# A decoder block's FFN output: two groups of nine pairs, with weight sums made ahead in device memory

## The chip, the cores and the metric

The kernel runs on one core of a Trainium2 chip. The metric is the device time of one launch in microseconds. Three runs of the kernel before gave a median of 2124.69 us (2124.45 to 2126.43). The engines are named as in the profile: PE is TensorE's matmul, PEld its weight load, DVE is VectorE, ACT is ScalarE, POOL is GpSimd and SP is SyncE. SP, ACT and POOL also issue DMA transfers, each on a queue of its own.

## The reference

With one layer the reference is a sparse-attention mixer and a SwiGLU FFN over 512 tokens of width 2048, with RMSNorm ahead of each and behind the last. The change is in the last part, the FFN's output and the final norm:

```python
x = x + nsa_mixer(rmsnorm(x, mix_norm_g), ...)           # (512, 2048)
h = rmsnorm(x, ffn_norm_g)
z = h @ w_in                                             # (512, 2 * 5632)
a, b = z[..., :5632], z[..., 5632:]
x = x + (silu(a) * b) @ w_out                            # (512, 5632) @ (5632, 2048)
return rmsnorm(x, final_norm_g)
```

All is float32. The kernel writes each operand as a sum of two float32r parts, high and low, and makes three matmuls of each product (`three`): high by high, high by low, low by high.

## The kernel before, in words

**Stages.** Attention, its output projection (`W_out`), the FFN input (`f_in`), the FFN output (`f_out`). An instruction's place in its engine's order is the order in which the Python code issues it. Splitting an operand takes one ACT copy (the high part) and one DVE subtraction (the low part, helper `sub`, line 1038).

**FFN input** (from about 864 us). 82 units `q`, two to each of 41 column blocks `p`. A unit is a product of the 2 by 2 blocks in seven products instead of eight (Strassen's way in Winograd's form): `split_unit` makes the sums of weight blocks and splits them, `load_unit(q + 3)` loads the weights of a later unit on SP's queue into three `raw` buffers and one `rawx`, `products(q)` issues 84 matmuls of 256 columns, `merge` puts the sums together. Each second `p` ends a pair: `merge` multiplies it by the gate of the block ahead, and `keep_a` stores 128 x 1024 numbers to `d_a` on POOL's queue. The tile that is stored, `E`, has two buffers.

**FFN output** (from about 1660 us). The sum over 5632 goes by 22 pairs `j` of 256, the columns by four blocks `b` of 512: 88 units (b, j), in the order of `ORDER`, block after block. Each block's sums stay in PSUM over its 22 units: four banks `po` and four `qs` for the parts of the seven products.

- A *plain* unit (`plain_tile`) loads its weights (512 KB) and its pair from `d_a` (512 KB, into `rawx` or `tt`), splits both (1024 columns each), and makes 24 matmuls of 512 columns, token tile by token tile.
- A *seven* unit (`seven_unit`, those in `SEVEN[b]`, 44 of the 88) takes seven products by 42 matmuls of 256 columns. Its left factors (four blocks of the pair and sums of them, in two parts of 1792 columns) are made by `form` during the four units ahead, and kept in SBUF for five pairs (`KEPT`); for the others they are stored to `d_s` and loaded again for each block on POOL's queue (`load_seven`). Its right factors are the four weight blocks and three sums of them, `weight_sums`: four DVE operations of 256 columns, and a split of 768.

`W2.take` gives a unit's split weights and splits those of units ahead. The split weights have four buffers, the split `thi`, `tlo` two. Where a seven unit follows a plain one, its split sums lie 32 columns further in their buffer than where it follows a seven (`c0`).

The residual stands in `d_r` and is loaded into `acc` (all four column blocks in SBUF). Behind the last seven unit of a block `merge_sums` adds the parts to `acc`; behind the block's last unit four additions do so with `po`. `ready(b)` then takes the block's sums of squares and multiplies it by the final gain, during the next block.

**The tail.** The last `N_TAIL` = 4 units of the last block are plain ones, taken token tile by token tile: for each tile four units' matmuls, then the addition to `acc` (line 954), sum of squares, gain (line 1559), the reciprocal root, and scaling and output of the four pieces. `last_tile` does the same for the last tile in two halves.

## Time and profile before

| | |
|---|---|
| median of 3 runs | 2124.69 us |
| profiled execution | 2123.49 us, span 2121.8 us, mean granted clock 0.998 |
| TensorE busy | 2098.6 us (99%), 14717 matmuls |
| VectorE busy | 1634.6 us (77%) |
| ScalarE busy | 932.7 us (44%) |
| DMA | 388.08 MB, mean 183 GB/s |

The span is cut into 40 slices of 53 us on the page; the FFN input takes slices 17 to 31 or so, the FFN output those behind. A busy TensorE is not a TensorE at its peak, since matmuls overlap; what one costs is read from the time between two starts. The lines that carry this are in the prediction.

### The profile page before, as it was taken

Reading aid. Unit: us, or ns where it says so; the run is one execution under the profiler, and the core shown is the slowest. Engines: PE = TensorE matmul, PEld = TensorE weight load, DVE = VectorE, ACT = ScalarE, POOL = GpSimd, SP = SyncE. Lnnn points to the kernel's source line nnn. Section 1 sums busy time; section 2 is a strip of 40 time slices with the busy share of each in tenths; the row PEclk is TensorE's granted clock in tenths of the full one; section 3 lists DMA queues with packets and bytes.
Section 4 is the critical chain, followed back from the end, with each engine's and each line's share of the span. In section 5 each row is a group of like instructions: output and inputs, shape, how many; then the busy total and the mean of one; then the engine's idle time right before and its main releaser. Section 6 shows DMA issues by size and latency. Waiting matters only on the chain.

```text
span 2121.8 us, 37227 instructions
## 1 busy us (share of the span) xinstructions
PE 2098.6 (99%) x14717; PEld 1947.1 (92%) x14717; DVE 1634.6 (77%) x2674; ACT 932.7 (44%) x1451; POOL 125.9 (6%) x206
## 2 busy tenths in 40 slices
PE   9999999999989999999999999999999999999998
PEld 7898788898979889999999999999999988999997
DVE  5565777877786366898888888888888787877785
ACT  5344455455554334434344343443434454444344
POOL 1000111111111000000000000000000000001000
PEclk9999999999999999999999999999999999999999
DMA  7555767666676643344344333434344776878893
GB/s 232 174 154 151 192 191 203 185 200 189 194 234 199 243 147 110 121 138 128 122 130 127 122 121 124 135 120 129 116 125 129 267 286 210 305 267 311 308 340 137
DMA packets 273371, 388.08 MB, mean 183 GB/s; under 512 B 34251, under 2 KB 206091, under 8 KB 272556
## 3 DMA queue, kind: packets, MB, share of 16 engines
q1 hardware_dynamic: 248540, 279.98, 42.3%
q0 software_dynamic: 22896, 102.31, 14.0%
q10 hardware_dynamic: 1760, 3.42, 0.4%
q8 instruction: 115, 1.88, 0.4%
q14 instruction: 60, 0.49, 0.1%
HBM read 320.52 MB, written 70.36 MB: 184 GB/s over the span
## 4 chain that ended last, share of the span: by engine, by line
PE 70%; ACT 0%; DVE 0%; issue 0%; ACTq 0%
PE f L268 19%; PE f L269 19%; PE f L270 19%; PE proj L268 2%; PE proj L269 2%; PE proj L270 2%; PE pp L268 1%; PE pp L270 1%; PE pp L269 1%; PE po L268 1%; PE po L269 1%; PE po L270 1%; PE pp L246 0%; PE o L269 0%; PE o L270 0%; PE o L268 0%
## 5 line engine op out<-in xcount | busy, mean ns | idle before, releaser
L98 DVE TENSOR_TENSOR wlo<-raw,whi 128x1024 fp32r<-128x1024 f32 (+1 forms) x225 | 269.3, 1199 | 116.2 <-ACT whi L97 115.9
L97 ACT ACTIVATE whi<-raw 128x1024 fp32r<-128x1024 f32 (+1 forms) x225 | 233.3, 1040 | 222.4 <-DVE raw L1038 123.2
L1038 DVE TENSOR_TENSOR tlo<-tt,thi 128x1536 fp32r<-128x1536 f32 (+2 forms) x135 | 197.1, 1460 | 109.0 <-ACT thi L1143 86.9
L270 PE MATMUL f<-hn_h,wlo 128*128 128x256 f32 x984 | 271.6, 276 | 0.0
L268 PE MATMUL f<-hn_h,whi 128*128 128x256 f32 x984 | 271.6, 276 | 0.0
L269 PE MATMUL f<-hn_l,whi 128*128 128x256 f32 x984 | 271.6, 276 | 0.0
L1138 ACT ACTIVATE whi<-raw 128x1024 fp32r<-128x1024 f32 x123 | 126.0, 1057 | 293.6 <-DVE raw L1038 290.2
L268 PE MATMUL proj<-hn_h,whi 128*128 128x512 f32 x512 | 204.2, 399 | 0.7 <-ACT hn_h L410 0.7
L269 PE MATMUL proj<-hn_l,whi 128*128 128x512 f32 x512 | 200.6, 392 | 0.3 <-DVE hn_l L411 0.3
L270 PE MATMUL proj<-hn_h,wlo 128*128 128x512 f32 x512 | 200.6, 392 | 0.0
L269 PEld LDWEIGHTS f<-hn_l,whi 128*128 128x128 f32 x984 | 184.7, 188 | 0.0
L268 PEld LDWEIGHTS f<-hn_h,whi 128*128 128x128 f32 x984 | 184.7, 188 | 0.0
L270 PEld LDWEIGHTS f<-hn_h,wlo 128*128 128x128 f32 x984 | 184.7, 188 | 0.0
L1143 ACT ACTIVATE thi<-tt 128x1536 fp32r<-128x1536 f32 x82 | 121.9, 1486 | 82.3 <-PE f L269 70.6
L270 PE MATMUL proj<-whi,hn_l 128*128 128x256 f32 (+2 forms) x496 | 145.4, 293 | 3.9 <-DVE hn_l L731 3.9
L1038 DVE TENSOR_TENSOR wlo<-raw,whi 128x1024 fp32r<-128x1024 f32 x123 | 147.0, 1223 | 1.1 <-ACT whi L1138 1.1
L268 PE MATMUL proj<-whi,hn_h 128*128 128x256 f32 (+2 forms) x496 | 145.7, 294 | 0.8 <-ACT hn_h L730 0.8
L269 PE MATMUL proj<-wlo,hn_h 128*128 128x256 f32 (+2 forms) x496 | 144.8, 292 | 0.0
L269 PE MATMUL f<-wlo,thi 128*128 128x512 f32 x320 | 124.9, 390 | 0.0
L270 PE MATMUL f<-whi,tlo 128*128 128x512 f32 x320 | 124.8, 390 | 0.0
L268 PE MATMUL f<-whi,thi 128*128 128x512 f32 x320 | 124.7, 390 | 0.0
L270 PEld LDWEIGHTS proj<-hn_h,wlo 128*128 128x128 f32 x512 | 96.4, 188 | 21.5 <-DVE wlo L98 0.2
(346 smaller groups left out, 6112.2 us busy)
## 6 DMA issues: line engine op xcount, KB each, us to landing
raw<-in_ffn_w_in SPq DMA_DIRECT2D x135, 512.0 KB, 3.7
raw<-in_ffn_w_out SPq DMA_DIRECT2D x88, 512.0 KB, 5.6
rawx<-in_ffn_w_in SPq DMA_DIRECT2D x41, 512.0 KB, 4.8
rawx<-d_a SPq DMA_DIRECT2D x31, 512.0 KB, 5.1
ah<-d_s POOLq DMA_DIRECT2D x16, 896.0 KB, 6.9
al<-d_s POOLq DMA_DIRECT2D x16, 896.0 KB, 9.3
raw<-in_nsa_w_in POOLq DMA_DIRECT2D x24, 512.0 KB, 4.8
raw<-in_nsa_w_in SPq DMA_DIRECT2D x23, 512.0 KB, 5.0
```

Of the source, the lines that this page charges most:

```text
L97: self.nc.scalar.activation(hi[:, :n], src, AF.Copy)
L98: self.nc.vector.tensor_tensor(lo[:, :n], src, hi[:, :n].bitcast(F32), op=OP.subtract)
L268: mm(o, ah, bh, start=start, stop=False, skip_group_check=True)
L269: mm(o, ah, bl, start=False, stop=False, skip_group_check=True)
L270: mm(o, al, bh, start=False, stop=stop, skip_group_check=True)
L1038: dve.tensor_tensor(o, a, b, op=OP.subtract)
L1138: act(h, r, AF.Copy)
L1143: act(h, ttf, AF.Copy)
```

## The change

- **Order.** `PASSES` replaces `ORDER`. Pairs 3 to 11 (`G1`) and 12 to 20 (`G2`) are the two groups. The first three passes take blocks 0, 1 and 2 over pairs 0 to 11 (in part), the fourth takes block 3 over both groups, and the last three take blocks 2, 1 and 0 over pairs 12 to 21 with the rest. The third part of each entry lists the pairs that are plain there; 63 units are seven units. At the end of a pass its block is added to `d_r` in device memory (first three) or the stored sum is added to it in SBUF and the block goes to `ready`, which now takes only the sums of squares and stores it (next three), both by an accumulating DMA on POOL's queue.
- **Left factors.** Each group's nine pairs keep their factors in 18 slots of SBUF (13 on the left side, five on the right). `form` is one generator run over two units: `form_front` issues the sums, `form_back` the ACT copies and, a unit later, the subtractions. The raw pair lands in the slot itself, two pairs ahead (`load_forms`). `d_s` and its traffic are gone.
- **Right factors.** `made_ahead` makes four sums of weight blocks for each of the 18 pairs and all four column blocks in device memory (`d_w`): four copies of 512 KB, then four accumulating transfers of 512 KB in three steps, all on POOL's queue. Its 72 steps are issued among the stages ahead: four beside `W_out`, six beside the first plain units of the FFN input, and three in each four of its units `q` (`PRE`). A seven unit loads 384 KB of plain weights and 512 KB of sums, two units ahead, and splits 768 and 1024 columns; DVE makes no sums of weights.
- **Tail.** Block 0 is the last. Its residual is added by an accumulating DMA into SBUF behind `merge_sums`, just ahead of the last four units. The other three blocks are read back to `ytile` (four loads of 768 KB), and each token tile is multiplied by their gain (1536 columns) in the tail.
- **Places.** New pools and gaps put slots and splits at the same offsets as before modulo 256 bytes.

The diff, cut to its core (left out are loads and splits that change their buffers alone, and names that follow):

```diff
-KEPT = (3, 8, 13, 16, 18)
-SEVEN = [KEPT + x for x in ((6, 11), (6, 11, 0, 1, 2, 4)) + 2 * ((6, 11, 0, 1, 2, 4, 5, 7),)]
-TAIL_LOAD, TAIL_SPLIT = {5: 0, 7: 1, 9: 2, 11: 3}, {7: 0, 9: 1, 13: 2, 15: 3}
-ORDER = [tuple(range(22)),
-         (3, 5, 6, 7, 0, 9, 8, 10, 1, 12, 11, 13, 14, 2, 16, 15, 17, 4, 18, 19, 20, 21),
-         (6, 9, 3, 11, 10, 5, 8, 12, 0, 13, 14, 1, 15, 7, 16, 2, 17, 18, 4, 19, 20, 21),
-         (6, 9, 11, 3, 0, 8, 1, 13, 2, 16, 4, 18, 5, 10, 7, 12, 14, 15, 17, 19, 20, 21)]
+G1, G2 = tuple(range(3, 12)), tuple(range(12, 21))
+PASSES = [(0, (6, 7, 8, 9, 3, 5, 4, 10, 11), (5, 6, 7, 8, 9, 10, 11)),
+          (1, (3, 4, 5, 6, 0, 7, 8, 9, 1, 10, 11), (0, 1, 10, 11)),
+          (2, (3, 4, 5, 6, 0, 7, 8, 9, 10, 11, 1), (0, 1)),
+          (3, (3, 4, 5, 0, 6, 7, 8, 1, 9, 10, 11, 12, 13, 2, 14, 15, 16, 17, 18, 19, 20, 21), (0, 1, 2, 21)),
+          (2, (12, 13, 14, 15, 16, 2, 17, 18, 19, 20, 21), (2, 21)),
+          (1, (12, 13, 14, 15, 16, 2, 17, 18, 19, 20, 21), (2, 21)),
+          (0, (12, 13, 14, 15, 16, 17, 18, 19, 20, 0, 1, 2, 21), (0, 1, 2, 21))]
+N_FIRST, FORM_FROM, PRE = 4, 2, (1, 1, 1, 0)
+UNITS = [(b, j, j not in flat) for b, js, flat in PASSES for j in js]
...
+    def three_of(j, b):
+        return (1, 768, [(0, 256, mat(f_out, 256 * j, 1, 512 * b, 256, D)),
+                         (256, 768, mat(f_out, 256 * j + 128, 1, 512 * b, 512, D))])
...
+    d_w = {j: dram.tile([128, 4, 4, 256], F32, name=f"d_w{j}") for j in G1 + G2}
+
+    def made_ahead():
+
+        for j in G1 + G2:
+            b11, b12, b21, b22 = (bass.AP(tensor=f_out.tensor, offset=f_out.offset + 128 * (2 * j + i) * D + 256 * c,
+                                          ap=[[D, 128], [512, 4], [1, 256]]) for i in range(2) for c in range(2))
+            t1, t3, t2, t4 = (d_w[j][:, :, i] for i in range(4))
+            for o, i in ((t1, b11), (t3, b12), (t2, b11), (t4, b21)):
+                pool.dma_start(o, i)
+            yield
+            pool.dma_start(t1, b12, accum_op=OP.add)
+            pool.dma_start(t3, b22, accum_op=OP.add)
+            yield
+            pool.dma_start(t2, t3, accum_op=OP.add)
+            yield
+            pool.dma_start(t4, t2, accum_op=OP.add)
+            yield
+
+    ready_made = made_ahead()
...
+            next(ready_made)
...
+                    if i != 1:
+                        next(ready_made)
...
+    def split_t(n):
+
+        def rest():
+            c0 = 0 if UNITS[n - 1][2] else 32
+            h, l = (tq.tile([128, 1088], F32R, name=f"t{x}")[:, c0:c0 + 1024] for x in ("hi", "lo"))
+            t = t_raw.pop(n)
+            act(h, t, AF.Copy)
+            sub(l, t, f32(h))
+            t_hl[n] = [x.rearrange("p (n c) -> p n c", n=4) for x in (h, l)]
+
+        return lambda r: rest
...
+        for _ in range(PRE[q % len(PRE)]):
+            next(ready_made, None)
+    run(ready_made)
...
+    def load_forms(n):
+
+        while len(raw_in) < min(len(used), forms["k"] + 2):
+            k = len(raw_in)
+            if k >= 9 and last_use[used[k - 9]] > n - 1 or k in (6, 7, 8) and n < N_FIRST:
+                break
+            raw_in.append((slot_tile(), slot_tile()))
+            nc.sync.dma_start(f32(raw_in[k][1][:, 768:]), d_a[used[k]])
...
+    def form_front(n, quiet):
+
+        k = forms["k"]
+        if forms["at"] or k >= len(used) or n < FORM_FROM:
+            return
+        must = first_use[used[k]] <= n + 2
+        if k >= len(raw_in) or quiet and not must:
+            return
+        forms["it"], forms["at"] = form(k), 1
+        next(forms["it"])
+
+    def form_back(n, quiet):
+
+        if forms["at"] == 1:
+            next(forms["it"])
+            forms["at"] = 2
+            if first_use[used[forms["k"]]] > n + 1:
+                return
+        elif quiet and forms["at"] == 2 and first_use[used[forms["k"]]] > n + 1:
+            return
+        if forms["at"] == 2:
+            next(forms["it"])
+            forms["at"] = 0
+            forms["k"] += 1
...
-        b = [[x[:, i, 256 * c:256 * (c + 1)] for x in w] for i in range(2) for c in range(2)]
-        th, tl = t_hl.pop(n)
-        right = dict(p1=b[0], p5=b[1], p2=b[2], p3=b[3], p7=(th[:, 0], tl[:, 0]), p6=(th[:, 1], tl[:, 1]),
-                     p4=(th[:, 2], tl[:, 2]))
-        for name in ("p7", "p6", "p1", "p5", "p2", "p3", "p4"):
+        t = t_hl.pop(n)
+        right = {p: [x[:, 0, 256 * i:256 * (i + 1)] for x in w] for i, p in enumerate(("p1", "p2", "p3"))}
+        right.update((p, [x[:, i] for x in t]) for i, p in enumerate(("p5", "p7", "p6", "p4")))
+        for name in ("p7", "p6", "p5", "p1", "p4", "p2", "p3"):
...
+    def merge_sums(qs):
+
+        o = accb["now"] = late2.tile([128, NT, 512], F32, name="accb")
+        u2 = late2.tile([128, 1024], F32, name="m")[:, :512]
 
         def halves(x):
             return x.rearrange("p (u c) -> p u c", u=2)
 
-        act(u3, qs["p1"], AF.Copy)
-        plus(u2, u3, qs["p6"])
-        plus(acc[:, :2, c[0]], acc[:, :2, c[0]], halves(u3))
-        plus(u3, u2, qs["p7"])
-        plus(acc[:, 2:, c[0]], acc[:, 2:, c[0]], halves(u3))
-        mm2 = m.rearrange("p (a c) -> p a c", a=2)
-        plus(mm2, mm2, qs["p5"].unsqueeze(1).to_broadcast([128, 2, 512]))
-        plus(acc[:, :, c[1]], acc[:, :, c[1]], m.rearrange("p (t c) -> p t c", t=4))
-
-    def ready(b, gf):
-
-        c = slice(512 * b, 512 * (b + 1))
+        act(o[:, :2, :256], halves(qs["p1"]), AF.Copy)
+        plus(halves(u2), o[:, :2, :256], halves(qs["p6"]))
+        plus(o[:, 2:, :256], halves(u2), halves(qs["p7"]))
+        sub(o[:, :2, 256:], halves(qs["p5"]), halves(u2))
+        sub(o[:, 2:, 256:], halves(qs["p5"]), o[:, 2:, :256])
+
+    def ready(b):
...
+        pool.dma_start(stored(b), o)
+
+    load_forms(0)
+    for i in range(2, N_FIRST + 1):
+        load_t(i)
+    load_a(N_FIRST)
...
+            load_forms(n)
+            form_front(n, quiet)
+            for x in range(W2.ncv, min(n + (4 if left == 0 else 3 if left < 3 else 2), NU)):
+                W2.ahead(x + 1 - W2.nt)
+                load_t(x + 2)
...
+            if last_pass and i == 6:
+                for t in range(NT):
+                    ytile[t] = slot_tile(F32)[:, 48:48 + 1536]
+                    nc.sync.dma_start(ytile[t], d_r[t][:, 512:])
+            if last_pass and i == 7:
+                gf = slot_tile(F32)[:, 48:48 + 512]
+                nc.sync.dma_start(gf, fin_g[None, :512].to_broadcast([128, 512]))
+                gfs = slot_tile(F32)[:, 48:48 + 1536]
+                nc.sync.dma_start(gfs, fin_g[None, 512:].to_broadcast([128, 1536]))
...
+        if last_pass:
+            merge_sums(pending)
+            pool.dma_start(accb["now"], stored(b), accum_op=OP.add)
+            continue
+        o = accb["now"]
+        for t in range(NT):
+            plus(o[:, t], o[:, t], po[t])
+        if s < 3:
+            pool.dma_start(stored(b), o, accum_op=OP.add)
+        else:
+            pool.dma_start(o, stored(b), accum_op=OP.add)
+            todo = ready(b)
...
+    for t in range(NT):
+        if t < NT - 1:
+            for i in range(N_TAIL):
+                if t == 0:
+                    w8.append(W2.take(N_TAIL - 1 - i))
+                plain_tile(n + i, w8[i], t, False, i == N_TAIL - 1)
+        dve.tensor_tensor(ytile[t], ytile[t], gfs, op=OP.mult)
+        if t == NT - 1:
+            break
+        plus(acc[:, t], acc[:, t], po[t])
+        act(po[t], acc[:, t], AF.Square, accum_out=ss[t][:, :1])
+        dve.tensor_tensor(acc[:, t], acc[:, t], gf, op=OP.mult)
...
```

More of the change, by code (lines that the diff above doesn't have):

```diff
@@ L164, in granules @@
         out += [(4, 256, [(0, 256, mat(f_in, 512 * i, 4, ffn_col(p), 256, 2 * DFF))]) for i in range(4)]
-    return out, [rows(f_out, 2 * j, 2, 512 * b, 512) for b in range(4) for j in ORDER[b]], marks, off
+    return out, [three_of(j, b) if seven else rows(f_out, 2 * j, 2, 512 * b, 512) for b, j, seven in UNITS], marks, off
 def ffn_col(p):
@@ L1306, in nsa_block, with load_a @@
-    for n, (b, j) in enumerate(seq):
-        if j in SEVEN[b]:
-            W2.sums[n] = weight_sums(n)
+    NU = len(UNITS)
+    a_raw, a_hl, t_raw, t_hl, slot = {}, {}, {}, {}, {}
+    tq = tp
+    plain_units = [n for n, (_, _, seven) in enumerate(UNITS[:-N_TAIL]) if not seven]
+    def load_a(i):
+        if i < len(plain_units):
+            n = plain_units[i]
+            a_raw[n] = (tp.tile([128, 1024 + 512 * (i % 2)], F32, name=("rawx", "tt")[i % 2], bufs=1)[:, :2 * S]
+                        if n < N_FIRST else tq.tile([128, 1024], F32, name="landp", bufs=1))
+            nc.sync.dma_start(a_raw[n], d_a[UNITS[n][1]])
@@ L1310, in nsa_block @@
+    def split_t(n):
[7 more added lines that the diff above has]
+        return lambda r: rest
+    for n, (_, _, seven) in enumerate(UNITS):
+        if seven:
+            W2.sums[n] = split_t(n)
     for q in range(NQ):
@@ L1333, in nsa_block @@
+    tq = ctx.enter_context(tc.tile_pool(name="tq", bufs=2))
     late2 = ctx.enter_context(tc.tile_pool(name="late2", bufs=1))
     ss = [late2.tile([128, 4], F32, name=f"sf{t}") for t in range(NT)]
[L1335 to L1340 removed]
@@ L1341, in nsa_block, with cols @@
[L1341 to L1352 removed]
+    accb, ytile = {}, {}
+    def cols(b):
+        return slice(512 * b, 512 * (b + 1))
@@ new lines, in stored, with slot_tile @@
+    def stored(b):
+        return d_r[:, :, cols(b)].rearrange("t p c -> p t c")
+    used = [j for js in (G1, G2) for j in js]
+    first_use = {j: n for n, (_, j, seven) in reversed(list(enumerate(UNITS))) if seven}
+    last_use = {j: n for n, (_, j, seven) in enumerate(UNITS) if seven}
+    n_slot = [0]
+    def slot_tile(dtype=F32R):
+        i = n_slot[0] % 18
+        n_slot[0] += 1
+        return (pair_pool if i < 13 else right).tile([128, 1792], dtype, name="slot", bufs=13 if i < 13 else 5)
@@ L1409, in plain_tile, with tail_load, tail_split @@
+    def tail_load(i):
+        n = NU - N_TAIL + i
+        a_hl[n] = [x[:, 48:48 + 2 * S] for x in (slot_tile(), slot_tile())]
+        nc.sync.dma_start(f32(a_hl[n][1]), d_a[UNITS[n][1]])
+    def tail_split(i):
+        h, l = a_hl[NU - N_TAIL + i]
+        act(h, f32(l), AF.Copy)
+        sub(l, f32(l), f32(h))
     def plain_tile(n, w, t, first, last):
@@ L1466, in nsa_block @@
         started = False
         for i, j in enumerate(units):
-            left = len(units) - 1 - i if b == 3 else 9
-            w = W2.take(3 if left == 0 else 2 if left < 3 else 1)
+            left = len(units) - 1 - i if last_pass else 9
+            quiet = i in (0, len(units) - 1) and not last_pass
+            load_forms(n)
[3 more added lines that the diff above has]
+                load_t(x + 2)
@@ L1502, in nsa_block, with piece @@
+        for t in range(NT):
[5 more added lines that the diff above has]
+            todo = ready(b)
+    acc = accb["now"]
     act(warm, epsc, AF.Sqrt)
-    def out_piece(t, c4, eng):
-        eng.dma_start(out[tok(t), c4], acc[:, t, c4])
+    def piece(t, b, c0=0, c1=512):
+        return acc[:, t, c0:c1] if not b else ytile[t][:, 512 * (b - 1) + c0:512 * (b - 1) + c1]
```

260 lines of the change are left out of this document (84 added, 176 removed).

## The prediction

> **What bounds the kernel now.** I read the front page first (busy shares and the slices), then the windows of the FFN stretch, then the waits of TensorE, then the DMA issues, and last the timelines of VectorE, SP and POOL at the places that the change touches. From the page:
>
> ```profile
> span 2121.8 us, 37227 instructions
> PE 2098.6 (99%) x14717; PEld 1947.1 (92%) x14717; DVE 1634.6 (77%) x2674; ACT 932.7 (44%) x1451; POOL 125.9 (6%) x206
> DVE  5565777877786366898888888888888787877785
> DMA  7555767666676643344344333434344776878893
> ```
>
> The profiled execution took 2123.49 us, 1.7 us beyond its span and 1.2 us under the median 2124.69; the sum below is made against 2123.49. TensorE is busy 99%, and DVE and the DMA engines are high in the last ten slices, the FFN output. The same stretch by windows (us, then busy time and instructions of each engine, clock, DMA share, GB/s):
>
> ```profile
> 864.00:1659.57 795.57, 795.57 (x6955) 793.04 (x6954) 682.88 (x805) 325.32 (x316) 11.30 (x22) 1.00 0.41 127
> 1659.57:1675.90 16.33, 16.33 (x75) 13.51 (x73) 14.43 (x23) 8.70 (x12) 1.29 (x2) 1.00 0.83 299
> 1675.90:1680.75 4.85, 4.85 (x44) 4.85 (x43) 3.39 (x6) 1.96 (x3) 0.00 (x0) 1.00 1.02 396
> 2020.45:2058.53 38.08, 38.08 (x339) 38.08 (x338) 33.29 (x51) 19.17 (x26) 4.20 (x8) 1.00 0.93 346
> 1659.57:2089.97 430.40, 430.40 (x2811) 391.85 (x2809) 343.94 (x493) 199.39 (x242) 28.26 (x52) 1.00 0.80 286
> 2089.97:2112.04 22.07, 22.07 (x121) 19.22 (x119) 11.57 (x34) 8.19 (x16) 0.00 (x0) 1.00 0.30 108
> ```
>
> The second window is three plain units (5.44 us each), the third one seven-product unit behind a plain one (4.85), the fourth eight seven-product units in a row (4.76 each), the fifth all units up to the last four, the sixth those four. The clock is 1.00 throughout. From 864 to 2112 TensorE's weight loads wait once:
>
> ```profile
> PEld f L270 <- DVE tlo L1038: 0.2, 1, 0.2
> ```
>
> So the stage is bound by the number of matmuls, and a unit turned from plain to seven products is worth its difference, so long as DVE (343.94 of 430.40 us, 80%) and the DMA engines (0.80) follow.
>
> **The units: minus 14.4 us.** Before, 44 of 88 units are seven-product; after, by the lists in PASSES, 63 (2+7+9+18+9+9+9). Up to the last four units, before has 40 plain and 44 sevens in 430.40 us. 19 of its sevens follow a seven (4.76) and 25 a plain unit (4.85), so the 40 plain ones took 430.40 - 90.4 - 121.3 = 218.7, or 5.47 each. After: 21 plain (114.8), 15 sevens that follow a plain unit (72.8), 48 that follow a seven (228.5): 416.0 us, 14.4 less. This takes it that long runs of sevens keep 4.76. At the 4.85 of a first unit everywhere, 48 x 0.09 = 4.3 us of it would go; since the new slots and splits lie multiples of 256 bytes apart, as the old ones do, I take 4.76.
>
> **DVE and ACT in the stage: nothing.** For a seven, DVE now does four 256-wide sums, a 1024-wide and a 768-wide subtraction:
>
> ```profile
> 2023.05 0.42 DVE L1038 TENSOR_TENSOR tt<-raw 128x256 f32<-128x256 f32 x1
> 2025.06 1.22 DVE L98 TENSOR_TENSOR wlo<-raw,whi 128x1024 fp32r<-128x1024 f32 x1 [0.34 <-ACT whi L97]
> 2026.33 0.96 DVE L1038 TENSOR_TENSOR tlo<-tt,thi 128x768 fp32r<-128x768 f32 x1
> ```
>
> That is 4 x 0.42 + 1.22 + 0.96 = 3.9 us. After, the four sums are gone (the DMA engines made them), and 0.96 (three direct blocks) + 1.22 (four made ones) = 2.2 us are left. A left factor costs 4 x 0.42 and subtractions of 256, 512 and 1024 (0.42 + 0.69 + 1.22), 4.0 us, spread over two units: 2.0 a unit. So in the densest stretch, the long pass over both groups, DVE has 4.2 us of work in 4.76, less than the 33.29 of 38.08 us it does in the eight units above, where TensorE waits for nothing. ACT has about 2.9 a unit in the same place (its splits are as wide, and a little shorter). The cover is one unit of splits made ahead; if it is gone, the first subtraction of a unit is late, and TensorE with it.
>
> Seven passes have six changes of pass instead of three, each with four 0.69 additions behind the last plain unit. Before shows no wait at its three, since each next pass opens with four products in other banks; all six do so after. Twelve multiplications by the gain (0.69 each) leave the stage and come back in the tail. The 32 reloads of stored factors on POOL's queue go; nothing but their own slots waited for them. Three plain units in a row at the end of the second pass share one landing buffer: split (2.5 us), then a load, must fit 5.44.
>
> ```profile
> raw<-in_ffn_w_in SPq DMA_DIRECT2D x135, 512.0 KB, 3.7
> raw<-in_ffn_w_out SPq DMA_DIRECT2D x88, 512.0 KB, 5.6
> rawx<-d_a SPq DMA_DIRECT2D x31, 512.0 KB, 5.1
> d_a<-E POOLq DMA_DIRECT2D x22, 512.0 KB, 2.9
> d_r<-acc POOLq DMA_DIRECT2D x4, 1024.0 KB, 4.1
> d_u<-d_t SPq DMA_DIRECT2D x16, 320.0 KB, 4.8
> acc<-d_r POOLq DMA_DIRECT2D x2, 1024.0 KB, 10.8
> ```
>
> 2.5 + 5.1 is 7.6, but the buffers let it begin up to a unit early; I count **1.5 us** for one or two short stalls (0 to 5, a late landing at each of five places). The stage's own traffic falls: 63 x 0.92 + 25 x 1.05 + 18 x 0.52 + about 15 MB of residual and gains is 108 MB, against 286 GB/s x 430 us = 123 MB. The residual's adds by DMA have most of a pass each, so nothing.
>
> **The sums made ahead: nothing, if they keep pace.** 18 pairs, each four copies of 512 KB from weight to device memory and then four accumulating transfers in three steps, all issued by POOL: 144 issues at 0.53 us. They run beside the FFN input, where the DMA engines are 0.41 busy. Two things can suffer. First the loads of input weights on SP's queue, which have this room:
>
> ```profile
> 1353.93 0.37 SPq L1121 DMA_DIRECT2D rawx<-in_ffn_w_in  x1
> 1368.87 0.69 DVE L1038 TENSOR_TENSOR tt<-rawx,raw 128x512 f32<-128x512 f32 x1
> 1362.45 0.53 POOL L1106 DMA_DIRECT2D d_a<-E  x1 [37.55 <-DVE E L1194]
> 1400.53 0.53 POOL L1106 DMA_DIRECT2D d_a<-E  x1 [37.55 <-DVE E L1194]
> ```
>
> The load issued at 1353.93 is read at 1368.87: 14.9 us, against 3.7 for a landing. A burst that halves its share makes it 7.4, still hidden. Second, what is queued behind a waiting accumulate on POOL: the store of the gated pair, one each 38.08 us (the two POOL rows), with three made-ahead steps between. Its buffer is wanted again one period later, so POOL may fall some 34 us behind in all before merging, then DVE and TensorE, wait. Three steps fit if a pair's four take under 4/3 x 38.08 = 50.8 us. No accumulate is in this trace. Low end: everything at the rate of the 512 KB load, 4 x 3.7 = 14.8 for the copies, and twice 3.7 for each accumulate, which has two operands to read (two together, then one, then one: 14.8 + 7.4 + 7.4), 44 us. High end: copies at the 4.8 us of the device-to-device row scaled to 512 KB (7.7 each, 31) and accumulates at the 10.8 us of the residual's load (21.6 + 10.8 + 10.8): 74 us. I take the low end, since the 10.8 us row was taken at 0.80 share, not 0.41.
>
> The Trainium skill, Collectives: The Full Stack, "Why ReduceScatter is half of AllGather", says that an add in the DMA engines costs nothing by itself but needs a second read, so it runs at half the rate of a copy. No run here shows it yet; it gives the low end again.
>
> **The tail: plus 6.6 us.** Rows of DVE around the last four units, and the width that is new there:
>
> ```profile
> 1347.07 1.76 DVE L1038 TENSOR_TENSOR tlo<-tt,thi 128x1536 fp32r<-128x1536 f32 x1 [0.25 <-ACT thi L1143]
> 2076.03 0.68 DVE L1041 TENSOR_TENSOR m<-m,f 128x512 f32<-128x512 f32 x1
> 2095.61 0.69 DVE L954 TENSOR_TENSOR acc<-acc,f 128x512 f32<-128x512 f32 x1 [3.12 <-PE f L270]
> 2099.13 0.88 DVE L1567 TENSOR_SCALAR acc<-acc,rs 128x512 f32<-128x512 f32 x2
> 2101.05 0.69 DVE L954 TENSOR_TENSOR acc<-acc,f 128x512 f32<-128x512 f32 x1 [1.03 <-PE f L270]
> 2111.15 0.72 ACT L1565 ACTIVATE acc<-acc,rs 128x512 f32<-128x512 f32 x1 [0.42 <-ACT acc L1565]
> 2110.81 0.15 DVE L1511 TENSOR_REDUCE part<-sf 128x1 f32<-128x3 f32 x1
> 2112.91 0.42 DVE L1041 TENSOR_TENSOR acc<-acc,f 128x256 f32<-128x256 f32 x1
> ```
>
> Now a token tile's chain takes 4.4 us of DVE's order (2095.61 to 2100.01) in a period of 5.44, with 1.03 idle. The change puts a 1536-wide multiplication by the gain (1.76) ahead of each: 6.16, so DVE becomes the limit. And the first chain now waits for more than matmuls: the block's merge comes behind the last seven (its fourth product ends 18 matmuls of 0.113, 2.0 us, before the tail starts; a copy of 0.72 and four additions of 0.69 end 1.6 us into it), and only then POOL fetches 1 MB of residual with an accumulate. Its landing lies between 4.1 us (the 1 MB store) and twice 10.8; I take 7.45, midway between the two 1 MB rows, as the loads have mostly stopped by then. So the first chain starts at 1.7 + 7.45 = 9.2 us instead of 5.5. Three chains and the multiplications behind each end 18.5 us later, at 27.6; the last tile's second addition follows 1.9 later (2112.91 - 2110.81, less 0.26 since the first addition is half as wide), at 29.5, where before has it at 2112.91 - 2089.97 = 22.9. **6.6 us** later, of which 2.9 are the multiplications and 3.7 the landing. Each us of landing beyond 4 moves the end by one; behind it all is as before.
>
> The slope of the two stores (2.9 us for 512 KB, 4.1 for 1 MB) leaves 1.7 fixed and 2.4 for 1 MB. By the Trainium skill's half rate, named above, the landing would be 1.7 + 4.8 = 6.5, and the sum one us better.
>
> **Sum.** -14.4 + 1.5 + 6.6 = -6.3 us: 2117.2 against 2123.49, or **2118.4** on the median's footing.
>
> **The rivals.**
> *POOL can't keep pace (slower).* From 50.8 us a pair on, POOL lags (pair time - 50.8) at each of 15.5 cycles, and past 34 us of lag the merge waits on the gated buffer: break-even at 53.0 plus what the units gain. At 56 us: 15.5 x 5.2 - 34 = 47 us lost, less 6.3: about 2165. For it: the high end 74, and that the loads share the same engines. Against: 0.59 of them idle there.
> *The tail eats the gain (no change).* Net gain is 13.8 minus the landing: a landing of 9.6 to 18 us leaves under 4.2 either way, 2120.5 to 2128.9, centre 2123. For it: 10.8 in the row above; against: 0.30 share in the last window.
> *The long runs of sevens don't hold 4.76.* With the third window's rate and a bit (4.93) in all 63, 10 us go: about 2128. For it: a first unit is 0.09 slower, so the rate depends on where data lies; against: eight in a row at 4.76.
> *Bursts delay the input loads (a loss).* Four copies land at once on the engines that feed the input stage. If they stretch a load of 3.7 us past its 14.9 us of room, each of 18 bursts stalls TensorE; at 0.9 us a burst that is 16 us, less 6.3: about 2134. For it: 2 MB in a burst, at the 127 GB/s of the first window, is 16 us of traffic. Against: a load would have to stretch fourfold. The Trainium skill, DMA: Bandwidth & Descriptors, "Issuing engines are not separate DMA queues", says that all queues interleave on the same 16 engines; the first window's 0.41 is the only sign of it here.
>
> **How the numbers follow.** A measurement of this kernel tells some 0.2%, 4.2 us. Forecast 0.64 (2110 to 2120.4); the tail or bursts give it back 0.18 (to 2128); slower 0.18, of which POOL's pace 0.09, the bursts 0.04 and the runs' rate 0.05. The range, 2110 to 2127, leaves out POOL's case and a little on both sides.
>
> **What would show it.** The page: PE's instructions up by 340, DVE's share down. Windows: runs of sevens at 4.76, the tail's start 13 us earlier. Waits: none of PE before the tail; on POOL, accumulates waiting for copies, and the store of the gated pair at its period of 38.08. DMA issues: accumulates of 512 KB under 8 us, the last 1 MB at 7.45. Timeline: DVE without gaps in the tail, the last addition 29.5 us after its start. Wrong would make it a growing period of the gated store, or a tail within 2 us of the present one (then 2113).

## Result: 21 us slower, and the profile after

The changed kernel takes 2146.28 us (median of 4 runs, 2145.87 to 2147.62) against 2125.02 for the kernel before on the same chip: 1.010 of its time, 95% interval 1.0083 to 1.0118. Forecast were 2118.4 us and a faster kernel. The profiled execution took 2147.62 us, span 2145.8, which is 24.0 us more than the span of before; what follows explains these 24.0 us.

The page after, the lines that answer to those of before:

```profile
PE 2096.8 (98%) x15059; PEld 1960.9 (91%) x15059; DVE 1585.7 (74%) x2541; ACT 938.9 (44%) x1469; POOL 231.8 (11%) x311
DMA  7555667666676667897796887878887677677776
raw<-in_ffn_w_in SPq DMA_DIRECT2D x135, 512.0 KB, 6.9
d_w<-in_ffn_w_out POOLq DMA_DIRECT2D x108, 512.0 KB, 10.3
tt<-d_w SPq DMA_DIRECT2D x64, 512.0 KB, 5.3
d_w<-d_w POOLq DMA_DIRECT2D x36, 512.0 KB, 7.8
```

TensorE issues 342 matmuls more and is busy 1.8 us less, so it idles 25.8 us longer. The DMA engines of the FFN input (slices 17 to 31) went from 3 or 4 tenths to 6 and more. The row of `d_w<-in_ffn_w_out` holds the 72 copies and the first two accumulates of each pair together. By windows (us, then busy time and instructions of each engine, clock, DMA share, GB/s), FFN input, output stage up to the tail, tail:

```profile
864.00:1663.52 799.52, 797.15 (x6952) 794.33 (x6950) 683.09 (x804) 324.55 (x316) 119.84 (x150) 1.00 0.81 210
1663.52:2104.63 441.11, 425.96 (x3152) 403.02 (x3151) 286.46 (x354) 205.14 (x259) 11.01 (x12) 0.98 0.74 234
2104.63:2145.80 41.17, 22.87 (x122) 19.15 (x120) 21.91 (x51) 11.22 (x26) 1.30 (x1) 0.86 0.57 186
```

Before, the FFN input ends at 1659.57, the output stage takes 430.40 us and the tail 31.83. So the 24.0 us are 3.95 in the FFN input, 10.71 in the output stage, 9.34 in the tail. DVE is less busy in the output stage (286 us against 344) and the DMA engines too (0.74 against 0.80): neither became the bound. What grew is the waiting of TensorE's weight loads, which was 0.2 us before. From 700 us to the end, the longest groups (us in total, times, the longest):

```profile
PEld f L296 <- DVE tlo L1067: 7.9, 2, 6.6
PEld f L296 <- DVE wlo L102: 5.9, 3, 2.6
PEld f L295 <- ACT whi L101: 2.4, 1, 2.4
PEld f L297 <- DVE slot L1067: 2.0, 1, 2.0
```

Taken unit by unit (from the first matmul of a unit to that of the next, in the timeline), the 84 units ahead of the tail take 416.6 us in their nominal times, 13.8 less than before, and 24.5 us in stalls. The stalls lie in six units of the first four passes, counted from 0 (us above the nominal time):

| unit | after | a_fm | b_wait | c_land | l_stage | what the wait ends with, in the kernel after |
|---|---|---|---|---|---|---|
| 3 | 4.97 | 0 | 4.08 | 0 | 0 | `fm` on the store of `E` |
| 9, 11 | 1.42 | 1.23 | 1.66 | 0 | 0 | `landp`, late for ACT |
| 12 | 3.79 | 5.92 | 4.97 | 0 | 0 | `tt`, late for ACT |
| 14 to 16 | 1.08 | 1.08 | 0.93 | 2.07 | 2.67 | a factor's last subtraction |
| 18, 19 | 4.37 | 4.96 | 0 | 0 | 0 | `landp`, late for ACT, then a form |
| 33 (35) | 8.84 | 8.89 | 0 | 10.69 | 0.57 | `fm` on the raw factor's load |
| all others | 0 | 0.87 | 0 | 1.36 | 1.91 | |
| sum | 24.47 | 22.95 | 11.64 | 14.12 | 5.15 | |

(The labels are those of the experiments below; l_stage is the three repairs together, and its "others" hold 0.93 in unit 0.) VectorE's timeline at units 3 and 33, the idle time before an operation and what ended it in brackets:

```profile
1679.67 0.76 DVE L1067 TENSOR_TENSOR fm<-slot 128x256 f32<-128x256 f32 x2 [7.60 <-DMA d_a<-E]
...
1838.44 1.22 DVE L1067 TENSOR_TENSOR tlo<-tt,thi 128x1024 fp32r<-128x1024 f32 x1
1849.48 0.76 DVE L1067 TENSOR_TENSOR fm<-slot 128x256 f32<-128x256 f32 x2 [9.81 <-DMA slot<-d_a]
1850.16 0.42 DVE L1067 TENSOR_TENSOR fm<-fm,slot 128x256 f32<-128x256 f32 x1
1850.61 0.42 DVE L1070 TENSOR_TENSOR fm<-slot,fm 128x256 f32<-128x256 f32 x1
1850.95 0.95 DVE L102 TENSOR_TENSOR wlo<-raw,whi 128x768 fp32r<-128x768 f32 x1
```

Both times DVE has nothing to do but a form that is not urgent, waits in it, and behind it in its order stand the splits that TensorE needs next. The load it waits for at 1849.48 was issued by SP at 1841.73, in the very unit in which DVE began the form:

```profile
1841.73 0.33 SPq L1377 DMA_DIRECT2D slot<-d_a  x1
```

ACT waits likewise at units 12 and 18, for tiles with one or two buffers:

```profile
1730.23 1.06 ACT L1309 ACTIVATE thi<-tt 128x1024 fp32r<-128x1024 f32 x1 [4.59 <-DMA tt<-d_w]
1765.34 1.06 ACT L1287 ACTIVATE thi<-landp 128x1024 fp32r<-128x1024 f32 x1 [4.58 <-DMA landp<-d_a]
```

Units 17 to 19 are the three plain units in a row. SP asks for the pairs of the last two 6.68 us apart, more than the 5.44 us of a plain unit, since one buffer must be split before it is loaded again; the loads themselves took 4.2 and 3.4 us. Behind that wait DVE is late, and 3.8 us of form work stand ahead of unit 19's splits:

```profile
1761.01 0.33 SPq L1282 DMA_DIRECT2D landp<-d_a  x1
1767.69 0.33 SPq L1282 DMA_DIRECT2D landp<-d_a  x1
```

```profile
1770.10 1.02 DVE L1067 TENSOR_TENSOR slot<-slot 128x256 fp32r<-128x256 f32 x2
...
1773.55 0.42 DVE L1070 TENSOR_TENSOR fm<-slot,fm 128x256 f32<-128x256 f32 x1
1773.89 1.22 DVE L102 TENSOR_TENSOR wlo<-raw,whi 128x1024 fp32r<-128x1024 f32 x1
```

The loads behind units 12 and 33 run beside the 1 MB accumulate of a pass's block into `d_r`, which POOL issued at 1720.67 and 1838.31 and which landed 13.5 and 11.7 us later. How much it delayed them no run here shows.

And a stall costs more than its idle time. The windows of unit 33: its wait, the 4.5 us behind it, the next 2.3:

```profile
1846.41:1853.20 6.79, 0.39 (x4) 0.19 (x2) 3.62 (x7) 3.07 (x5) 0.00 (x0) 0.83 0.45 112
1853.20:1857.70 4.50, 4.50 (x21) 4.50 (x22) 4.43 (x5) 1.55 (x2) 0.00 (x0) 0.50 0.89 264
1857.70:1860.00 2.30, 2.30 (x22) 2.30 (x21) 0.39 (x2) 1.06 (x1) 0.00 (x0) 1.00 1.03 352
```

Behind the wait 21 matmuls take 4.50 us at a granted clock of 0.50, then 22 take 2.30 at 1.00. Of the 24.5 us, the gaps between matmuls are 18.0; the other 6.5 are nearly all matmuls at half rate.

The tail (POOL's and VectorE's timelines):

```profile
2106.68 1.30 POOL L1543 DMA_DIRECT2D accb<-d_r  x1 [29.09 <-DVE accb L1067]
```

```profile
2110.87 1.23 DVE L102 TENSOR_TENSOR wlo<-raw,whi 128x1024 fp32r<-128x1024 f32 x1 [4.84 <-ACT whi L101]
2112.89 1.76 DVE L1609 TENSOR_TENSOR slot<-slot 128x1536 f32<-128x1536 f32 x1 [0.80 <-DMA slot<-in_final_norm_g]
2117.88 0.69 DVE L1070 TENSOR_TENSOR accb<-accb,f 128x512 f32<-128x512 f32 x1 [3.23 <-DMA accb<-d_r]
```

The residual is asked for at 2106.68 and landed at 2117.8, 11.1 us later; the first addition stands 13.25 us into the tail, the last 32.6.

In the FFN input one load was late: from 864 us four copies and two accumulates are issued by POOL, and VectorE then waits 4.70 us for `rawx`, which was issued at 871.22 and took 15.6 us to land:

```profile
886.94 0.69 DVE L1067 TENSOR_TENSOR tt<-rawx,raw 128x512 f32<-128x512 f32 x1 [4.70 <-DMA rawx<-in_ffn_w_in]
```

### The profile page after: what moved, and what is told of

Its sections match the earlier page's. It is cut to its first block, busy times and chain, and to the rows that moved or that the text cites. A ratio compares the mean times of both kernels' runs of the same rounds, so it can differ in the third digit from the quotient of the medians.

```text
span 2145.8 us, 38164 instructions
## 1 busy us (share of the span) xinstructions
PE 2096.8 (98%) x15059; PEld 1960.9 (91%) x15059; DVE 1585.7 (74%) x2541; ACT 938.9 (44%) x1469; POOL 231.8 (11%) x311
## 5 line engine op out<-in xcount | busy, mean ns | idle before, releaser
L1067 DVE TENSOR_TENSOR tlo<-tt,thi 128x1536 fp32r<-128x1536 f32 (+1 forms) x147 | 223.7, 1522 | 164.7 <-ACT thi L1309 95.4
L102 DVE TENSOR_TENSOR wlo<-raw,whi 128x1024 fp32r<-128x1024 f32 (+2 forms) x225 | 252.4, 1125 | 109.3 <-ACT whi L101 108.2
L101 ACT ACTIVATE whi<-raw 128x1024 fp32r<-128x1024 f32 (+2 forms) x225 | 219.2, 977 | 95.4 <-PE po L297 26.8
L296 PE MATMUL f<-tlo,slot 128*128 128x256 f32 x504 | 141.6, 281 | 7.4 <-DVE tlo L1067 7.4
L297 PE MATMUL f<-thi,slot 128*128 128x256 f32 x504 | 141.4, 281 | 2.5 <-DVE slot L1067 1.8
L295 PE MATMUL f<-thi,slot 128*128 128x256 f32 x504 | 141.1, 280 | 0.0
L1309 ACT ACTIVATE thi<-tt 128x1024 fp32r<-128x1024 f32 x63 | 67.0, 1063 | 165.7 <-PE f L297 65.4
```

What stands on the lines that cost most here:

```text
L101: self.nc.scalar.activation(hi[:, :n], src, AF.Copy)
L102: self.nc.vector.tensor_tensor(lo[:, :n], src, hi[:, :n].bitcast(F32), op=OP.subtract)
L295: mm(o, ah, bh, start=start, stop=False, skip_group_check=True)
L296: mm(o, ah, bl, start=False, stop=False, skip_group_check=True)
L297: mm(o, al, bh, start=False, stop=stop, skip_group_check=True)
L1067: dve.tensor_tensor(o, a, b, op=OP.subtract)
```

## Experiments

The theory: the whole loss is a few late landings, each of which VectorE or ScalarE awaits in its order with urgent work behind, and the half rate that follows. The rival: with the sums ahead and more loads, the DMA engines are full, and a stall that is removed comes back elsewhere.

The experiments ran on three chips, on which the kernel before took 2126.17 us (a_fm, b_wait, c_land, e_spread), 2125.67 (j_added, d_gain, d_both, g_all) and 2127.29 (the others); beside the result above it took 2125.02. Each ratio is to the kernel before on the same chip. The changed kernel was not run there again, so a difference to its 2146.28 us can be off by the 1 to 2 us that lie between these times. Stalls and stages are read from one profiled execution of each kernel.

**a_fm: the form's scratch tile in another pool.**

```diff
-        m = late2.tile([128, 1024], F32, name="fm").rearrange("p (n c) -> p n c", n=2)
+        m = tq.tile([128, 1024], F32, name="fm", bufs=1).rearrange("p (n c) -> p n c", n=2)
```

> Edit: the small tile fm, which holds a form's first sum, comes from the pool that holds tt, not from the pool that is laid over the memory of the gated stores' tile E. Theory (a few late landings on which DVE's order waits): the first fm operation of the stage no longer waits for the store of E, so the weight gap before the 4th unit (index 3, 4.97 us above its nominal time) goes, and the kernel is 4 to 5 us faster than the changed kernel, about 2141.5; the later gaps stay. Rival (the DMA engines are full there, and the gap only moves to the next late landing): the 4th unit is as late by its slot's landing or another tile's, and the time stays within 1.5 us of 2146.3.

2146.04 us (2139.42 to 2148.61), ratio to before 1.0086 (1.0066 to 1.0107). VectorE's first `fm` operation has no wait now:

```profile
1674.20 0.75 DVE L1067 TENSOR_TENSOR fm<-slot 128x256 f32<-128x256 f32 x2
```

Unit 3's 4.97 us are gone, as the theory has it. The median did not fall: it lies where the rival put it, and the profiled execution is the slowest of the four (2148.61). In it unit 12 took 2.1 us more, and the FFN input ended 2.2 us later. The latter is not a wait but 256-wide matmuls that start every 0.118 us instead of 0.113, some 4% slower, for about 140 us (windows of this run; 342 and 353 matmuls in 40 us):

```profile
940.00:980.00 40.00, 40.00 (x342) 40.00 (x341) 32.98 (x39) 15.80 (x17) 6.20 (x8) 1.00 0.82 219
1020.00:1060.00 40.00, 40.00 (x353) 40.00 (x352) 34.42 (x41) 15.50 (x15) 4.74 (x5) 1.00 0.76 177
```

In every profiled execution, that of the kernel before too, the first 256-wide matmuls of the FFN input start every 0.118 us, up to about 888 us. In some (here, d_gain, d_both and k_nospread) this lasts to about 1028 us and costs about 5 us; so the starts of the output stage are not to be compared between runs, and what follows goes by stage.

**b_wait: a form begins two units after its load.** `raw_at` notes the unit in which a raw pair was asked for.

```diff
+            raw_at.append(n)
...
-        if k >= len(raw_in) or quiet and not must:
+        if k >= len(raw_in) or (quiet or n < raw_at[k] + 2) and not must:
```

> Edit: a pair's form is begun only once its raw factor was asked for at least two units before. Theory: the form of the 10th factor, which DVE began in the unit in which its load was issued, no longer holds the splits of the 34th unit behind a landing of 9.8 us; the gap before that unit (8.84 us with its half-clock part) goes, and the time is 8 to 9 us below the changed kernel's 2146.3, about 2137.7. Rival (the factor is needed at that time and the landing only moves): the form's end is now what the 12th pair's first use waits for, and at most 2 us are won.

2135.91 us, ratio 1.0047 (1.0032 to 1.0062): 10.4 us below the changed kernel. VectorE's `fm` there now waits 1.65 us, and TensorE not at all:

```profile
1846.06 0.76 DVE L1067 TENSOR_TENSOR fm<-slot 128x256 f32<-128x256 f32 x2 [1.65 <-DMA slot<-d_a]
```

The 8.84 us went, and with them the 4.37 of unit 19. There the two loads of `landp` are still asked for 6.25 us apart and ACT waits 6.28 us for one, but no new form stands ahead of unit 19's splits: that stall took both, the late pair and the form. The twelfth pair's first use is not late: the rival fails.

**c_land: one ring of three landing tiles.** Pairs and sums land in the same three buffers, loaded in the order of the units; the loads asked for ahead of the first unit are dropped.

```diff
-                        if n < N_FIRST else tq.tile([128, 1024], F32, name="landp", bufs=1))
+                        if n < N_FIRST else tq.tile([128, 1024], F32, name="land", bufs=3))
...
-            t_raw[n] = tq.tile([128, 1024], F32, name="tt", bufs=2)
+            t_raw[n] = tq.tile([128, 1024], F32, name="land", bufs=3)
...
+        elif N_FIRST <= n < NU - N_TAIL:
+            load_a(plain_units.index(n))
...
-    for i in range(2, N_FIRST + 1):
-        load_t(i)
-    load_a(N_FIRST)
```

> Edit: one ring of three landing tiles for whole pairs and for sums, loaded in the order of the units, in place of two for sums and one for pairs. Theory (single landing tile reused too late): the ACT waits for landp and tt before units 9, 12, 16 and 19 go, worth together 1.42 + 3.79 + 1.08 + 4.37 = 10.7 us with what the half clock adds; since the forms' own landings remain just in time, 4 to 8 us of it are expected, about 2140. Rival (DMA engines are full while the sums ahead are made, so a transfer asked for earlier also lands later): no more than 2 us are won.

2134.90 us, ratio 1.0040 (1.0026 to 1.0054): 11.4 us below the changed kernel, more than expected. Units 9, 12 and 19 lost their stalls (9.6 us); unit 3's went too, since the store of `E` landed in 6.1 us, not 9.5; unit 16's, which was to go too, stayed (2.07 in units 14 to 16); unit 33 got 1.9 worse, and this execution had no late `rawx`. With the same bytes to move, loads that are asked for earlier land earlier: this is what the rival denied.

**j_added: the sums ahead alone, in the kernel before.** `made_ahead` and its calls are added and `d_w` is never read.

```diff
+    d_w = {j: dram.tile([128, 4, 4, 256], F32, name=f"d_w{j}") for j in G1 + G2}
+    ready_made = made_ahead()
...
         products(q)
+        for _ in range(PRE[q % len(PRE)]):
+            next(ready_made, None)
```

> Edit: the kernel before, with the changed kernel's sums ahead (18 pairs of 4 copies and 4 accumulates on POOL) added and never read; the output stage is the old one. Theory (the added transfers delay input loads only at the burst of 864 to 890 us, by 4 us and not in every execution): up to 4 us slower than before, 2125 to 2130, with the FFN input stage the only place. Rival (the engines are full, and that is what the output stage's late landings come from): the old output stage, which is still beside the transfers' end at its start, is also later, and the time is 2135 or more.

2126.42 us against 2125.67, ratio 1.0004 (0.9994 to 1.0014): they cost nothing that can be told from the noise, at most 3 us by the interval. The windows of its FFN input and output stage:

```profile
864.00:1661.16 797.16, 796.88 (x6959) 793.99 (x6958) 682.40 (x805) 323.23 (x316) 120.13 (x151) 1.00 0.82 211
1661.16:2090.00 428.84, 427.45 (x2793) 388.67 (x2792) 345.13 (x495) 198.91 (x242) 28.34 (x52) 1.00 0.81 286
```

Its DMA engines are as full as in the changed kernel or fuller (0.82 and 0.81 against 0.81 and 0.74), and TensorE idles 1.7 us in all. Full DMA engines by themselves are not the cause; the rival fails.

**e_spread: the four copies two and two.** A pair has five steps then, and one is issued in each unit of the FFN input.

```diff
-N_FIRST, FORM_FROM, PRE = 4, 2, (1, 1, 1, 0)
+N_FIRST, FORM_FROM, PRE = 4, 2, (1, 1, 1, 1)
...
-            for o, i in ((t1, b11), (t3, b12), (t2, b11), (t4, b21)):
-                pool.dma_start(o, i)
+            pool.dma_start(t1, b11)
+            pool.dma_start(t3, b12)
             yield
             pool.dma_start(t1, b12, accum_op=OP.add)
             pool.dma_start(t3, b22, accum_op=OP.add)
             yield
+            pool.dma_start(t2, b11)
+            pool.dma_start(t4, b21)
+            yield
```

> Edit: the four 512 KB copies of a pair's sums are issued two and two, with the first two accumulates between, where the changed kernel issues all four at once. Theory (bursts of POOL's transfers beside an input load): the wait of 4.70 us for rawx at 886.9 us goes and the FFN input stage is 4 us shorter, so the output stage starts at about 1659.5 and the time is about 2142.3. Rival (the transfers' mean share of the engines, not their order, is what delays loads): the stall stays or comes at another pair, and the time is within 1.5 us of 2146.3.

2147.75 us, ratio 1.0099 (1.0084 to 1.0114). The wait for `rawx` is gone and the output stage starts at 1659.86, 3.7 us earlier, as expected; but its stalls are 28.2 us, 3.7 more (2.0 of them in unit 12, 1.6 in three late units of 0.4 to 0.8), and the tail is 1.2 longer. The expected total was missed, and the measured one lies where the rival put it (within 1.5 us of 2146.3): what one place gained, others lost. Whether the new order did that is not shown, since unit 12's stall lies between 3.8 and 5.9 us in all the kernels that keep it.

**d_gain and d_both: the tail.** First the gain goes back into `ready` (blocks 1 to 3), then block 0's residual also comes by SP ahead of time.

```diff
+        g = late2.tile([128, 512], F32, name="gfb")               # in ready(b)
+        nc.sync.dma_start(g, fin_g[None, cols(b)].to_broadcast([128, 512]))
...
+            dve.tensor_tensor(o[:, t], o[:, t], g, op=OP.mult)
...
-        dve.tensor_tensor(ytile[t], ytile[t], gfs, op=OP.mult)     # in the tail
...
-            pool.dma_start(accb["now"], stored(b), accum_op=OP.add)
+            for u in range(2):
+                plus(accb["now"][:, 2 * u:2 * u + 2], accb["now"][:, 2 * u:2 * u + 2], res[u])
```

> Edit: the gain of blocks 1 to 3 is multiplied in ahead of the last pass, as in the kernel before, and the four 128x1536 gain products of the tail go; the accumulate stays. Theory (DVE sets the tail's end once the last accumulate has landed; each product there is some 1.8 us and one or two of them stand ahead of or between the additions): the last addition moves from 32.6 us into the tail to 28 to 30, and the time is 2141 to 2144. Rival (the accumulate's landing sets everything): the products fill only time in which DVE waits anyway, and the time is within 1.5 us of 2146.3.

> Edit: as the run before in this list (gain products out of the tail), and block 0's residual is loaded by SP units ahead into two slots and added by DVE (two adds of 128x2x512) in place of the 1 MB accumulate that took 11.1 us. Theory: the first normalised addition no longer waits 13.25 us into the tail but about 5, the last addition comes at 22 to 25 us into it, and the time is 2136 to 2139. Rival (the last matmuls' weight split behind other loads sets the end, or DVE's additions do): 2141 or more.

2146.43 us, ratio 1.0099 (1.0084 to 1.0114), and 2150.37 us, 1.0113 (1.0098 to 1.0128). Both miss the expected total, and both lie where their rival put it. The tail itself went from 41.2 to 35.7 us in both: with d_gain the last addition stands 27.2 us into it (28 to 30 expected), and the accumulate lands in 8.4 us, beside fewer loads. Without the accumulate nothing more is won. VectorE in d_both's tail, which starts at 2112.56:

```profile
2116.06 2.35 DVE L1070 TENSOR_TENSOR accb<-accb,slot 128x1024 f32<-128x1024 f32 x2
2118.33 1.22 DVE L102 TENSOR_TENSOR wlo<-raw,whi 128x1024 fp32r<-128x1024 f32 x1
2122.14 0.69 DVE L1070 TENSOR_TENSOR accb<-accb,f 128x512 f32<-128x512 f32 x1 [2.59 <-PE f L297]
```

The additions that replace the accumulate stand ahead of the last weights' split, TensorE waits for that, and the first addition comes at 9.6 us, not 5: the rival of d_both. The totals are no better because the edit made a stall of its own in unit 80 (6.5 and 5.9 us, a gain row asked for too late; below), and both profiled executions had the slow stretch in the FFN input.

**l_stage: the three repairs of the output stage together** (the edits of a_fm, b_wait and c_land).

> Edit: only the three repairs in the output stage (fm, forms two units after their load, one ring of three landings); the tail and the sums ahead are the changed kernel's. Theory (stalls of the stage are worth 24.5 us, of which the three take 20 to 22; the tail's 9.3 us stay): 2124 to 2128, level with the kernel before. Rival (the repairs overlap, or a stall moves into the last passes): 2131 or more.

2125.92 us, ratio 0.9998 (0.9989 to 1.0008), as expected. Its output stage takes 19.9 us less than the changed kernel's. Its windows, output stage and tail:

```profile
1660.53:2081.79 421.26, 418.38 (x3152) 396.79 (x3151) 288.80 (x356) 204.75 (x260) 11.00 (x12) 1.00 0.77 244
2081.79:2123.20 41.41, 24.21 (x122) 20.19 (x120) 21.92 (x51) 11.18 (x26) 1.30 (x1) 0.83 0.56 182
```

The output stage is 421.26 us, 9.1 below the kernel before, at the same traffic; the tail gives it back.

**g_all, k_early, k_nospread: all repairs.** g_all has the five above; k_early asks for the gain row at the end of the pass before; k_nospread is k_early with the copies issued at once. The edit from g_all to k_early:

```diff
         else:
             pool.dma_start(o, stored(b), accum_op=OP.add)
-            todo = ready(b)
+            g = late2.tile([128, 512], F32, name="gfb")
+            nc.sync.dma_start(g, fin_g[None, cols(b)].to_broadcast([128, 512]))
+            todo = ready(b, g)
```

> Edit: the five repairs together (fm out of the pool over E, forms begun two units after their load, one ring of three landings, gain and residual out of the tail, copies spread). Theory (a few late landings, each with its half-clock part, are the whole loss): the output stage takes its 416.6 us of units and at most 5 us of stalls, the tail 33 or less, and the time is 2112 to 2118, faster than before. Rival (DMA engines full, stalls move): at 2125 or more it is no better than before.

> Edit: the five repairs together, and the gain row that DVE waited 5.62 us for in the last pass is asked for at the end of the pass before, not three units later. Theory: the 6.19 us that its unit (index 80) stood above its nominal time go, nothing else moves, and the time is 2113 to 2116 against 2120.6 with the five alone. Rival (another load of the last pass is late in its place): 2118 or more.

> Edit: as the run before in this list, but with the four copies of a pair issued at once, as in the changed kernel. Theory (the spread moved the end of the transfers later and gained nothing by itself): within 2 us of the version with the spread. Rival (the FFN input stage's stall of 4 us, or a long stretch of matmuls at 0.118 in place of 0.113 us, comes back): 3 to 6 us above it.

g_all: 2120.58 us, ratio 0.9976 (0.9965 to 0.9987), faster than before, so the rival fails; it is short of the expected 2112 to 2118 by the stall of unit 80, here 6.19 us:

```profile
2061.32 0.69 DVE L1485 TENSOR_TENSOR accb<-accb,gfb 128x512 f32<-128x512 f32 x1 [5.62 <-DMA gfb<-in_final_norm_g]
```

k_early: 2118.86 us (2114.43 to 2120.42) against 2127.29, ratio 0.9957 (0.9945 to 0.9969). Unit 80's stall is gone, but the expected 2113 to 2116 is missed, and the rival came true: another load of the last pass is late. ACT waits 4.03 us for late weights, the last split stands behind the residual's additions, TensorE waits 2.69 us for it (1.00 in g_all), half rate follows, and the tail takes 35.8 us (g_all 32.7). On this chip the kernel before took 1.6 us longer than on that of g_all, so the gain over g_all is larger in the ratios than in the times. k_nospread: 2120.72 us, 0.9963 (0.9949 to 0.9977), within the 2 us that the theory gave, but its ten runs scatter from 2114.68 to 2128.16 us, and the profiled one (2127.26) has the slow stretch that the rival named. That stretch came in four of the nine profiled executions that issue the copies at once and in none of the three that spread them; that the spread prevents it is not shown. k_early beats both kernels, the one before by 0.4%. Its output stage:

```profile
1661.34:2081.28 419.94, 417.62 (x3153) 396.66 (x3151) 290.62 (x364) 202.29 (x258) 10.99 (x12) 1.00 0.78 245
```

**h_stalls: waits of graded length in the kernel before.** Extra additions on VectorE ahead of seven units.

```diff
+STALL = {10: 3, 20: 4, 30: 5, 40: 6, 50: 7, 60: 8, 72: 9}
...
+            if n in STALL:
+                idle = late2.tile([128, 1024], F32, name="m")
+                dve.memset(idle, 0.0)
+                for _ in range(STALL[n]):
+                    plus(idle, idle, idle)
```

> Edit: the kernel before, with 3 to 9 extra DVE additions of 128x1024 (some 1.2 us each) ahead of the work of seven units of the output stage, so that TensorE waits for ever longer. Theory (an idle of about 1.7 us or more is followed by some 4 us of matmuls at half rate, an idle of 1.2 us or less by none): the units with a long gap lose their gap and 2 us more, and the granted clock of the 4 us behind it is about 0.5; those with a short gap lose only the gap. Rival (the half rate follows from the number of late weights, not the idle): gaps of 2 us and more without a half-rate stretch behind them.

2181.98 us (one run). Gaps from 1.70 us (with one of 0.91 behind it) to 9.14 us came, each followed by half rate, so the rival fails. The gaps add up to 43 us of the some 55 by which this run is longer, which leaves about 1.7 us behind each of the seven. The windows behind the shortest and behind one of 3.62 us:

```profile
1728.00:1730.00 2.00, 2.00 (x7) 1.57 (x6) 1.93 (x5) 0.74 (x1) 0.00 (x0) 0.55 1.03 321
1730.00:1732.00 2.00, 2.00 (x7) 1.56 (x6) 1.67 (x3) 2.00 (x5) 0.00 (x0) 0.60 0.87 333
1732.00:1734.00 2.00, 2.00 (x10) 1.63 (x9) 1.97 (x6) 0.83 (x1) 0.00 (x0) 1.00 0.71 214
...
1845.00:1847.00 2.00, 2.00 (x11) 2.00 (x11) 1.60 (x5) 1.30 (x2) 0.00 (x0) 0.50 0.22 83
```

No short gap came in this run, so the expectation's other half is read from the others: d_gain and d_both had two gaps in unit 3, 1.08 + 0.90 and 0.93 + 0.90 us. The windows of 2 us behind them, d_gain's and then d_both's:

```profile
1686.00:1688.00 2.00, 2.00 (x7) 1.51 (x6) 1.97 (x4) 1.94 (x4) 0.00 (x0) 0.50 0.54 131
```

```profile
1686.00:1688.00 2.00, 2.00 (x11) 1.64 (x10) 1.97 (x4) 2.00 (x4) 0.00 (x0) 1.00 0.54 135
```

1.98 us of waiting brought the half rate, 1.83 us did not; a single gap of 1.2 us (c_land, unit 16) did not either, and a single one of 2.08 us did (the changed kernel, unit 12: a granted clock of 0.53 from 1734.70 to 1736.70). These are single executions: they bound no limit.

## Why the prediction was wrong, by its steps

On the profiled executions the forecast was -14.4 + 1.5 + 0 + 6.6 = -6.3 us, and measured were -13.8 (units), +24.5 (stalls of the stage), +3.95 (FFN input) and +9.3 (tail), 24.0 in all.

- **The units: right.** 416.6 us in nominal times, 13.8 less than before (14.4 forecast). Runs of sevens hold 4.76, so the rival of their rate fell.
- **DVE and ACT in the stage: the step that failed.** The price was 1.5 us for short stalls, and 24.5 came. The work was weighed rightly (DVE has room: 286 us of 441); the order was not. The step put median landings against free time, where the question was, at each new wait, what stands behind it on its engine. Three things were missed: `fm` comes from a pool that takes over the memory of `E`, and waits for its last store; a form could begin in the unit of its load; and a wait has a price behind it, 6.5 us of the 24.5. A fourth was seen and priced too low: the three plain units with one landing buffer were named, but "the buffers let it begin up to a unit early" did not hold (6.68 us between two loads, in units of 5.44), and with a form ahead of the next splits that place lost 4.37 us. The accumulates at the ends of passes were put at "nothing" too; they ran beside the loads that were late for units 12 and 33, and their share stays open. a_fm, b_wait and c_land each took away the stalls that they were made for (c_land not unit 16's), b_wait that of unit 19 and c_land that of unit 3 besides, and l_stage all but 5.2 us.
- **The sums made ahead: right in the mean.** They cost nothing that can be told from the noise in the kernel before (j_added), and POOL kept its pace, though an issue took it 1.02 us in the median (line 221) and not 0.53. The row of the gated store among the instructions on the tile `E`, from 900 us on:

```profile
L1135 POOL DMA_DIRECT2D d_a<-E x20: 565/581/590, 912.9 to 1633.0; - x20
```

  19 periods in 720.1 us are 37.9 each, so the rival of POOL's pace fell. The rival of the bursts was seen once (4.70 us at 886.94, behind a load that took 15.6 us and had been given 14.9), not at each of 18. The median landing of `raw<-in_ffn_w_in` rose from 3.7 to 6.9 us, and the 14.9 us of room covered that. The Trainium skill, DMA: Bandwidth & Descriptors, "Issuing engines are not separate DMA queues", says that transfers of all queues interleave on the same 16 engines. These landings agree.
- **The tail: right in kind, too small.** 9.3 us longer, 6.6 forecast. The term that was mis-sized is the landing: 11.1 us instead of 7.45, so the first addition came at 13.25 instead of 9.2; the tiles then follow at 6.04 (6.16 forecast). The other estimate, 6.5 by the half rate, was further off. The assumption that "the loads have mostly stopped" was wrong: the last weights, the last of four loads of 768 KB and the gain land behind 2106.68. The condition of the rival "the tail eats the gain", a landing of 9.6 to 18 us, came true, and l_stage, with this tail and few stalls, is level with the kernel before.
- **The sum.** Repaired (k_early), the same change takes 8.4 us off the kernel before on the same chip, where 6.3 was forecast. That is no proof of the forecast but partly luck: the repairs also took some 5 us off the changed kernel's tail.

The Trainium skill, TensorE: Matmul & The Clock Gate, "What's actually happening", gives half rate after an idle window of about 3.4 us and full rate after as long a busy one. The stretch of half rate agrees (3 to 4.5 us in the windows above). The idle that brings it does not: 2.08 us in one piece (unit 12), and 1.98 us in two, were enough here.

## What to carry to other kernels

When a change adds loads or moves them closer to their use, ask for each new wait what stands behind it in that engine's order; work that isn't urgent must not begin before its data has surely landed, or it holds up what is. Give each landing its room from the longest landing beside a burst, not from the median, and count behind each stall of 2 us or more about 1 to 2 us of slow matmuls. The share of busy DMA engines tells nothing about this: it was 0.74 in the output stage with the stalls, and 0.77 to 0.81 in those nearly without.

## What was not expected of the hardware

- A wait of TensorE of 2.08 us, and two that together took 1.98 us, put its clock at 0.50 for some 3 us; 1.83 us in two did not (one execution each).
- The 256-wide matmuls of the FFN input follow each other at 0.118 us up to about 888 us in every kernel and then at 0.113, both at a granted clock of 1.00. In four executions, all of kernels with the sums ahead, they stay at 0.118 for about 140 us more, and 5 us are lost; the cause stays open.
- A 1 MB accumulate into SBUF took 11.1 us in the tail and 8.4 us there beside fewer loads. In the median, accumulates of 512 KB in device memory took 7.7 and 7.9 us where they were issued alone, and 10.0 and 13.1 where two were issued together; the copies, four at once, took 9.9.
